# A hybrid decoder block on one core: all four compute engines run in the order written, and the attention's values move between pairs two and three

## The chip, the cores and the metric

The kernel runs on one core of one Trainium2 chip. The metric is the device time of one execution in microseconds (us). The core's engines have a queue of instructions each: TensorE (PE, matmuls; its weight loads are counted apart as PEld), VectorE (DVE), ScalarE (ACT), GpSimd (POOL) and SyncE (SP, which here only issues transfers). An engine works through its queue in the order in which the built program holds it; semaphores make it wait for others. PSUM is the memory that PE writes and that DVE and ACT read.

## What is computed

One layer, 256 tokens of width 1024. A norm, one projection to all streams, two token mixers side by side (softmax attention with 8 heads, and the RWKV-7 delta rule with 8 heads of 64), gates, and one output projection with a norm:

```python
h = rmsnorm(x, norm_pre[l])
proj = jnp.einsum('bsd,de->bse', h, w_in[l])
aq, ak, av, az, rw_stream, rz, g_att, g_rw = split_cols(proj, IN_WIDTHS)
ya = moba_attention(heads_a(aq), heads_a(ak), heads_a(av)) * silu(az)
rs, ksr, vs, wd, ad = split_cols(token_shift_mix(rw_stream, rw_mu[l]), ...)
w_log = -softplus(-(rw_w0[l] + tanh(wd) @ rw_w_up[l])) - 0.5
a = sigmoid(rw_a0[l] + ad @ rw_a_up[l])
...
# rwkv7_scan, for each token: S_t = S_{t-1} diag(w_t) + (S_{t-1} (-kk_t)) (kk_t * a_t)^T + v_t k_t^T ; o_t = S_t r_t
u = sigmoid(g_att) * (ya @ w_up_att[l]) + sigmoid(g_rw) * (yb @ w_up_rw[l])
x = x + rmsnorm(u @ w_out[l], norm_post[l])
```

With 256 tokens there is one block of keys, so the attention is causal softmax attention with ALiBi.

## The kernel before

The weights lie in DRAM as blocks of 128x1024 in the order in which they are used. Each block is loaded to `wraw` (SP queue), cast to a rounded high part `whi` on ACT (L123), and the rest `wlo` is the difference, made on DVE (L124). A block of output features is then 24 matmuls of 128x256 in triples (L137 to L139): high weights times high input, high times low, low times high. `wblock` keeps four split blocks ready, so the split of block n+3 is written at the start of block n. There are four buffers for each part, so that split waits until PE is through with block n-1.

Beside this stream run the small products of the two mixers, as generators in three lanes: `rw` (lora, the four pairs of RWKV heads, the inverse, the chunks), `att` (scores, softmax, values) and `nm` (norms of the chunks). In `proj_tile` there are three marks in each block (after k = 2, 4 and 7), at which `pump` gives every lane its rate, and a lane whose credit reaches 1 runs its next generator to the next `yield`. R_SUB, R_ATT and R_CH are such rates; a `yield` alone is one more step, so a step without work puts distance between a product and its inputs.

The stages: the opening (input norm, transposes, first three blocks, L150 to L215), wda and lora, then for p in 0 to 3 the blocks k, r and v of a pair. `pair_phase` (L373 to L438) makes decays by a scan (L378) and exps (L381, L384), the operands kap, km, ar, BK and rk, the bonus product L407, the products L422 to L427, and copies them out through masks (L434). Then the attention's values (`av_phase`, L613), eight blocks for q and k with the scores L629 between, twelve for the gates and z, four for the attention's gate. `inverse_phase` inverts 64 matrices of 32x32 at once, one substitution step (L478, L480) for each row, and moves the result through DRAM (dx, dt) into X64; L501 and L511 complete it. `chunks_phase` then runs four chunks in sequence: L524, L552, L562, L539.

What sets the order: only the opening stands under `manual_schedule`, where ACT, DVE, PE and POOL keep the order in which the code is written. For the rest a scheduler orders each engine's instructions by its own estimate of when they are ready, with a raised priority for the weight splits, the shifts and the evacuations (`hp`).

```python
cast = nc.scalar.copy(out=hi[:, a:b], in_=raw[:, a:b])
nc.vector.tensor_tensor(out=lo[:, a:b], in0=raw[:, a:b], in1=hi[:, a:b], op=ALU.subtract)
```

Of the kernel before, what the change touches and what calls it, by code (L numbers as in the profile page):

```python
# [16 lines left out]
P = 128  # L17
# [10 lines left out]
DMA_SLOTS, DMA_SLOTS2 = 10, 16  # L28
# [4 lines left out]
R_ATT, R_SUB, R_CH = 0.107, 0.75, 0.8  # L33
# [10 lines left out]
def block_kernel(ctx: ExitStack, tc: tile.TileContext, x, wp, pv, lora, npost, out):  # L44
# [102 lines left out]
    first = [wfetch(halves=n == 0) for n in range(4)]  # L147
    started = [mmps() for _ in range(3)]
    ET = mybir.EngineType
    with tc.manual_schedule(engines={ET.Activation, ET.DVE, ET.PE, ET.Pool}):  # L150

        for i in range(2):
# [5 lines left out]
            normed = nc.gpsimd.tensor_tensor(out=r, in0=r, in1=mhalf[:, 0:1], op=ALU.pow)  # L158
# [7 lines left out]
        x_scale(0, 0, 512, nc.vector)  # L166
        x_scale(0, 512, D, nc.scalar)
        x_scale(1, 0, 384, nc.vector)
        x_scale(1, 384, 768, nc.scalar)
        x_scale(1, 768, D, nc.vector)  # L170
        omu = ct([P, 13], "omu")
        nc.vector.tensor_scalar(out=omu, in0=pvt[:, PV_MU:PV_MU + 13], scalar1=-1.0, scalar2=1.0, op0=ALU.mult, op1=ALU.add)
        oka = ct([P, 4], "oka")
        nc.vector.tensor_scalar(out=oka, in0=pvt[:, PV_KA:PV_KA + 4], scalar1=-1.0, scalar2=1.0, op0=ALU.mult, op1=ALU.add)
        two = twops()
        banks = [two[:, 0], two[:, 1]] + [smps() for _ in range(3)]
        place = [(0, 0), (1, 0), (2, 0), (2, 1), (3, 0), (3, 1), (4, 0), (4, 1)]
        xps = [banks[b][:, h * T:(h + 1) * T] for b, h in place]

        def x_tr(i, j):  # L180
            nc.tensor.transpose(out=xps[j][:, i * P:(i + 1) * P], in_=xt[i][:, j * P:(j + 1) * P], identity=ident)

        def x_evac(j):
            nc.scalar.activation(out=hh[:, j, :], in_=xps[j], func=AF.Identity, scale=pvc(PV_NPRE, j))
            nc.vector.scalar_tensor_tensor(out=hl[:, j, :], in0=xps[j], scalar=pvc(PV_NPRE, j), in1=hh[:, j, :],  # L185
                                           op0=ALU.mult, op1=ALU.subtract)

        def mm_hi(n, k):
            ws = first[n][1][:, k * P:(k + 1) * P]
            nc.tensor.matmul(out=started[n][:, 0:T], lhsT=ws, rhs=hh[:, k, :], start=(k == 0), stop=False)  # L190
            nc.tensor.matmul(out=started[n][:, 0:T], lhsT=ws, rhs=hl[:, k, :], start=False, stop=False)  # L191
# [6 lines left out]
        for i in range(2):  # L198
            for j in range(KD):
                x_tr(i, j)  # L200
        nc.vector.tensor_copy(out=first[0][1][:, 0:512], in_=first[0][0][:, 0:512])
        for j in range(5):
            x_evac(j)
            mm_hi(0, j)
            if j == 1:
                nc.vector.tensor_copy(out=first[0][1][:, 512:D], in_=first[0][0][:, 512:D])
        nc.scalar.copy(out=first[1][1], in_=first[1][0])
        for j in range(5):
            mm_hi(1, j)
        for j in range(5, KD):  # L210
            x_evac(j)
            mm_hi(0, j)
            mm_hi(1, j)
        nc.scalar.copy(out=first[2][1], in_=first[2][0])
        mm_lo(0)  # L215
        for k in range(KD):
            mm_hi(2, k)
        mm_lo(1)
        mm_lo(2)
        split_3 = wsplit(first[3], 0, 1024)  # L220
    ready.append(first[3][1:])
    nc.sync.dma_start(out=lor, in_=lora.rearrange("r (n c) -> r n c", n=2))
# [68 lines left out]
    bonv = ct([P, NP, T], "bonv")  # L291
    nc.gpsimd.memset(SVE[0:64, 0], 0.0)
# [5 lines left out]
    rnt = ct([P, NP, NCH], "rnt")  # L298
# [74 lines left out]
    def pair_phase(p):  # L373

        k2 = tg()
# [6 lines left out]
        nc.gpsimd.tensor_copy(out=Gc[:, p], in_=Gl[:, :, C:C + 1])  # L382
# [21 lines left out]
        yield  # L404
        mm = nc.tensor.matmul
# [27 lines left out]
        for sc, kd, sct, kr in ((scs[:, 0], ARE, SCE, LH[1]), (scs[:, 1], ARO, SCO, LH[0])):  # L433
# [14 lines left out]
    def inverse_phase():  # L448

        dn = dram.tile([64, 32, 32], F32, name="dn")  # L450
        dx, dt_ = (dram.tile([64, 32, 32], F32, name=n) for n in ("dx", "dt"))
        for q in range(4):
            o = 32 * (q % 2)
            nc.sync.dma_start(out=dn[16 * q:16 * q + 16].rearrange("b s t -> s b t"),
                              in_=[SCE, SCO][q // 2][32 * q:32 * q + 32, :, :, o:o + 32].rearrange("s p c t -> s (p c) t"))
        nc.vector.reciprocal(out=rn2, in_=rn2)
        nc.vector.tensor_copy(out=rnt[0:64], in_=rn2[:, 0])
        nc.sync.dma_start(out=rnt[64:128], in_=rn2[:, 1])
# [6 lines left out]
        fl = tt([P, 32, 32], "slot")[0:64]  # L465
        nc.gpsimd.dma_start(out=fl, in_=dn)
        tb = tt([P, 32, 32], "slot")[0:64]
        nc.gpsimd.memset(tb, 0.0)
        nc.gpsimd.memset(tb.rearrange("b s t -> b (s t)")[:, 0:1024:33], 1.0)
        for c in range(DMA_SLOTS):  # L470
            if c < NCH - 1:
                bkt_phase(c)
            yield
# [8 lines left out]
        yield 1.0  # L482
        xb = tt([P, 32, 32], "slot")[0:64]
# [62 lines left out]
    def chunks_phase():  # L546
# [3 lines left out]
        for c in range(NCH):  # L550
            u = p4(smps())
            one_group([mm(out=u[fs, p, :], lhsT=X64[fs, p, c, :], rhs=wsb[fs, p, :], start=True, stop=True)  # L552
                       for p in range(NP) for h, fs, AR, SV, UV, SC in (EV, OD)])
            for h, fs, AR, SV, UV, SC in (EV, OD):
                nc.vector.tensor_tensor(out=UV[fs, c], in0=u[fs], in1=rnt[fs, :, c:c + 1].broadcast_to([64, NP, C]), op=ALU.mult)
# [8 lines left out]
            for h, fs, AR, SV, UV, SC in (EV, OD):  # L564
                gc = Gc[fs, :, c, :].broadcast_to([64, NP, C])
# [31 lines left out]
    yah = ct([P, NP, T], "yah", F32R)  # L597
    yal = ct([P, NP, T], "yal", F32R)
# [164 lines left out]
    def main():  # L763
# [28 lines left out]

        zg = ct([P, 3, NP, T], "BK")
# [5 lines left out]
        att.drain()  # L799
        for p in range(NP):  # L800
# [3 lines left out]
            split(at, yah[:, p, :], yal[:, p, :])  # L804
# [13 lines left out]
        for j in range(0, KD, 2):  # L818
# [3 lines left out]
            up_pair(j, yah, yal, up_att_done)  # L822
# [70 lines left out]
    finish(1, 3)  # L893


def pack(inputs):
# [11 lines left out]
    blocks += [wide(w, 1024, b) for b in range(4)]  # L908
# [44 lines left out]
```

## Time and profile before

| | before |
|---|---|
| median of 3 runs | 255.26 us (254.19 to 256.28) |
| the profiled execution | 255.23 us |
| its span, first to last instruction | 253.5 us |
| mean granted clock of PE | 0.983 |
| PE busy | 238.7 us |
| DVE / ACT / POOL busy | 181.2 / 149.4 / 32.8 us |

The span is the time from the first to the last instruction of the core; the 1.7 us around it are start and end. Busy is the union of an engine's instructions, and a matmul's record is longer than its distance to the next one, since they are pipelined. The clock is granted at one of two levels, 1.2 and 2.4 GHz, told as 0.5 and 1.0. In the row of waits, "PE smps L407 <- DVE gen L403" says that PE stood before its L407, which writes a PSUM tile named smps, until DVE had done L403.

### The profile page before, as it was taken

To read this page: it belongs to the slowest core of one execution; us is meant where nothing else is said; L and a number is where in the kernel's file an instruction comes from. 1 tells how busy PE (TensorE), PEld (TensorE's weight loads), DVE (VectorE), ACT (ScalarE), POOL (GpSimd) and SP (SyncE) were. 2 spreads that over 40 slices of the span, in tenths; PEclk is the share of its full clock that TensorE was granted. 3 is DMA by queue.
4 is the path that set the end of the run, shared out by engine and by line. 5 is a ranking of instruction groups with operands and counts; after the bars stand their busy time and mean duration, and the time that the engine had idled before them with its cause. 6 is when DMAs were issued, how large, how long until landed. Compare 5 with 4: busy or idle time off the path is not lost.

```text
span 253.5 us, 5779 instructions
## 1 busy us (share of the span) xinstructions
PE 238.7 (94%) x2283; PEld 220.8 (87%) x2283; DVE 181.2 (72%) x370; ACT 149.4 (59%) x291; POOL 32.8 (13%) x74
## 2 busy tenths in 40 slices
PE   8799998799999999999999999999997999999990
PEld 5599998798879899989899999899896999988890
DVE  2677747789894256999999277987777666998243
ACT  4676899286553767778598565763334443573241
POOL 2735000012120520000001500000112100000000
PEclk9979999799999999999999999999999999999998
DMA  6825955956578692552625958334226566442022
GB/s 231 352 67 153 376 176 175 263 177 178 125 193 257 145 356 89 172 165 87 202 100 162 272 160 288 130 107 155 82 78 217 211 200 206 168 152 98 3 74 93
DMA packets 19500, 43.68 MB, mean 172 GB/s; under 512 B 7536, under 2 KB 8688, under 8 KB 19472
## 3 DMA queue, kind: packets, MB, share of 16 engines
q1 hardware_dynamic: 18336, 41.30, 50.4%
q0 software_dynamic: 704, 1.71, 2.6%
q8 instruction: 18, 0.29, 0.5%
q10 hardware_dynamic: 432, 0.29, 0.4%
q14 instruction: 10, 0.08, 0.1%
HBM read 37.90 MB, written 1.84 MB: 157 GB/s over the span
## 4 chain that ended last, share of the span: by engine, by line
PE 78%; DVE 8%; ACT 5%; issue 4%; DMA 2%; POOL 1%; DVEq 0%; SPq 0%; ACTq 0%; POOLq 0%
PE mmps L137 17%; PE mmps L138 16%; PE mmps L139 16%; PE mmps L853 9%; PE mmps L613 3%; DVE wlo L124 2%; ACT whi L123 2%; DMA slot<-in_x_dram 2%; PE mmps L191 1%; PE twops L629 1%; PE smps L654 1%; POOL rv L581 1%; PE smps L663 1%; PE mmps L190 1%; PE twops L422 1%
## 5 line engine op out<-in xcount | busy, mean ns | idle before, releaser
L137 PE MATMUL mmps<-hh,whi 128*128 128x256 f32 x336 | 96.6, 288 | 2.2 <-DVE k L274 2.2
L139 PE MATMUL mmps<-hh,wlo 128*128 128x256 f32 x336 | 95.1, 283 | 0.0
L138 PE MATMUL mmps<-hl,whi 128*128 128x256 f32 x336 | 95.1, 283 | 0.0
L124 DVE TENSOR_TENSOR wlo<-wraw,whi 128x1024 fp32r<-128x1024 f32 x58 | 71.3, 1232 | 25.2 <-ACT whi L123 25.1
L123 ACT CAST whi<-wraw 128x1024 fp32r<-128x1024 f32 x58 | 60.8, 1048 | 41.6 <-PE mmps L138 26.7
L137 PEld LDWEIGHTS mmps<-hh,whi 128*128 128x128 f32 x336 | 63.9, 190 | 3.5 <-DVE k L274 2.4
L138 PEld LDWEIGHTS mmps<-hl,whi 128*128 128x128 f32 x336 | 63.9, 190 | 0.3
L139 PEld LDWEIGHTS mmps<-hh,wlo 128*128 128x128 f32 x336 | 63.8, 190 | 0.2
L478 DVE SCALAR_TENSOR_TENSOR gen<-slot,rnf 64x31 f32<-64x31 f32 (+15 forms) x31 | 12.2, 392 | 0.7
L480 DVE TENSOR_TENSOR slot<-slot,gen 64x31 f32<-64x31 f32 (+15 forms) x31 | 10.4, 334 | 0.7
L581 POOL TENSOR_TENSOR rv<-rv,mhalf 128x4 f32<-128x4 f32 x4 | 4.2, 1052 | 41.8 <-DVE rv L580 41.8
L137 PE MATMUL mmps<-yah,whi 128*128 128x256 f32 x32 | 9.2, 287 | 0.0
L139 PE MATMUL mmps<-slot,wlo 128*128 128x256 f32 x32 | 9.1, 283 | 0.0
L137 PE MATMUL mmps<-slot,whi 128*128 128x256 f32 x32 | 9.1, 283 | 0.0
L138 PE MATMUL mmps<-slot,whi 128*128 128x256 f32 x32 | 9.1, 283 | 0.0
L139 PE MATMUL mmps<-yah,wlo 128*128 128x256 f32 x32 | 9.0, 281 | 0.0
L138 PE MATMUL mmps<-yal,whi 128*128 128x256 f32 x32 | 9.0, 281 | 0.0
L859 DVE TENSOR_TENSOR SCE<-mmps,X 128x512 f32<-128x512 f32 (+1 forms) x5 | 2.9, 584 | 8.2 <-ACT ar L858 8.2
L858 ACT ACTIVATE ar<-mmps 128x512 f32<-128x512 f32 (+1 forms) x5 | 2.6, 514 | 10.2 <-PE mmps L853 10.2
L191 PE MATMUL mmps<-hl,whi 128*128 128x256 f32 x24 | 7.7, 343 | 0.6 <-DVE hl L185 0.2
L190 PE MATMUL mmps<-hh,whi 128*128 128x256 f32 x24 | 7.7, 341 | 0.2
L191 PEld LDWEIGHTS mmps<-hl,whi 128*128 128x128 f32 x24 | 5.5, 229 | 1.4 <-DVE hl L185 1.4
(260 smaller groups left out, 498.7 us busy)
## 6 DMA issues: line engine op xcount, KB each, us to landing
wraw<-in_wp_dram SPq DMA_DIRECT2D x64, 512.0 KB, 3.9
slot<-in_x_dram SPq DMA_DIRECT2D x2, 512.0 KB, 4.0
wraw<-in_wp_dram SPq DMA_DIRECT2D x2, 256.0 KB, 5.5
gz<-in_lora_dram SPq DMA_DIRECT2D x1, 512.0 KB, 8.2
ARE<-ar SPq DMA_DIRECT2D x4, 128.0 KB, 3.2
ARO<-ar SPq DMA_DIRECT2D x4, 128.0 KB, 3.2
bonv<-gen SPq DMA_DIRECT2D x8, 64.0 KB, 2.8
ARE<-SCE SPq DMA_DIRECT2D x4, 128.0 KB, 2.3
```

The costliest lines, as they stand in the source:

```text
L123: cast = nc.scalar.copy(out=hi[:, a:b], in_=raw[:, a:b])
L124: nc.vector.tensor_tensor(out=lo[:, a:b], in0=raw[:, a:b], in1=hi[:, a:b], op=ALU.subtract)
L137: nc.tensor.matmul(out=o, lhsT=lh, rhs=rh, start=first, stop=False)
L138: nc.tensor.matmul(out=o, lhsT=lh, rhs=rl, start=False, stop=False)
L139: nc.tensor.matmul(out=o, lhsT=ll, rhs=rh, start=False, stop=last)
L190: nc.tensor.matmul(out=started[n][:, 0:T], lhsT=ws, rhs=hh[:, k, :], start=(k == 0), stop=False)
L191: nc.tensor.matmul(out=started[n][:, 0:T], lhsT=ws, rhs=hl[:, k, :], start=False, stop=False)
L478: nc.vector.scalar_tensor_tensor(out=pr, in0=fl[:, s, s + 1:32].unsqueeze(2).broadcast_to([64, n, s + 1]), scalar=rnf[:, s:s + 1], in1=tb[ ...
L480: nc.vector.tensor_tensor(out=tb[:, s + 1:32, 0:s + 1], in0=tb[:, s + 1:32, 0:s + 1], in1=pr, op=ALU.add)
L581: nc.gpsimd.tensor_tensor(out=rv, in0=rv, in1=mhalf, op=ALU.pow)
L613: nc.tensor.matmul(out=pa[i], lhsT=a[:, k, ts], rhs=w[:, wsl], start=(k == 0 and n == 0), stop=(k == KD - 1 and n == 2))
L853: nc.tensor.matmul(out=ps, lhsT=a[:, k, ts], rhs=w[:, wsl], start=(k == 0 and m == 0), stop=(k == KD - 1 and m == 2))
```

## The change

Everything after the opening comes under `manual_schedule` too, for ACT, DVE, PE and POOL (SP's transfers are still ordered by the scheduler). So the order of the code becomes the order of the queues, and the generators are cut finer: more `yield`s, other rates. R_PAIR (0.9 of a step for each mark) is new, R_ATT rises from 0.107 to 0.16, R_SUB from 0.75 to 0.8, and R_CH falls from 0.8 to 0.5. The slots that separate the inverse's parts go from 10 and 16 to 8 and 9. The attention's values (the four wide blocks) follow pair 1 instead of pair 3, and `rw.drain()` before the inverse is gone. Line numbers shift: L378 is L400 after the change, L403 is L425, L407 is L430, L422 is L446, L434 is L458, L446 is L481, L480 is L515, L484 is L521, L501 is L535, L524 is L557, L552 is L585.

Beside the order:
- the opening is written in other steps (both norms first, four groups of features, six small bf16 products `keep_warm` between the first transposed features);
- the lora's tanh is written by ACT into both halves, where two transfers moved one half before, and its split moves from POOL to DVE;
- `Gc` is made by an exp on ACT instead of a copy on POOL;
- the masked diagonal blocks go to DRAM (`dn`) pair by pair, 16 transfers instead of 4;
- BK of the first three chunks is scaled by the decay, 12 activations of 128x192 (L471), so that the state update becomes one addition to `dec`, made earlier; in chunk 0 it is a copy;
- the norm factors `rnt` are gone: one multiply L519 (64x1024) puts them into the inverse, and the two multiplies at L496 and the factor in L555 go;
- the chunk's u has a PSUM tile for each half of the heads.

```diff
-DMA_SLOTS, DMA_SLOTS2 = 10, 16
+DMA_SLOTS, DMA_SLOTS2 = 8, 9
-R_ATT, R_SUB, R_CH = 0.107, 0.75, 0.8
+R_PAIR, R_ATT, R_SUB, R_CH = 0.9, 0.16, 0.8, 0.5
...
+        def keep_warm():
+            nc.tensor.matmul(out=started[2][:, 0:T], lhsT=wz[:, 0:P], rhs=wz, start=True, stop=True)
...
     def pair_phase(p):
+        if p == 0:
+            yield R_PAIR
...
-        nc.gpsimd.tensor_copy(out=Gc[:, p], in_=Gl[:, :, C:C + 1])
+        nc.scalar.activation(out=Gc[:, p], in_=c4(cs)[:, :, C - 1:C], func=AF.Exp, scale=-DECAY_SCALE)
...
         nc.vector.scalar_tensor_tensor(out=rk, in0=rs_[p], scalar=pvc(PV_RK, p), in1=km, op0=ALU.mult, op1=ALU.mult)
+        yield
         yield
...
+            nc.sync.dma_start(out=dn[16 * q + 4 * p:16 * q + 4 * p + 4].rearrange("b s t -> s b t"),
+                              in_=[SCE, SCO][q // 2][32 * q:32 * q + 32, p, :, o:o + 32])
+    def bk_decay(c):
+        for p in range(NP):
+            nc.scalar.activation(out=BK[:, p, c, :], in_=BK[:, p, c, :], func=AF.Identity, scale=Gc[:, p, c, :])
...
         for c in range(DMA_SLOTS):
             if c < NCH - 1:
-                bkt_phase(c)
+                bk_decay(c)
+            if 2 <= c < NCH + 1:
+                bkt_phase(c - 2)
+            if c == NCH:
+                bkt_done.append(c)
             yield
...
+        nc.vector.tensor_tensor(out=tb, in0=tb, in1=rnf.unsqueeze(2).broadcast_to([64, 32, 32]), op=ALU.mult)
         xb = tt([P, 32, 32], "slot")[0:64]
         nc.vector.tensor_copy(out=xb, in_=tb.rearrange("b t j -> b j t"))
...
-            u = p4(smps())
+            ue, uo = p4(smps()), p4(smps())
...
-                nc.vector.tensor_tensor(out=dst, in0=s[fs], in1=SV[fs, c], op=ALU.add)
-                nc.vector.tensor_tensor(out=dst, in0=dst, in1=gc, op=ALU.mult)
+                if c:
+                    nc.vector.tensor_tensor(out=dst, in0=s[fs], in1=dec[fs], op=ALU.add)
+                else:
+                    nc.vector.tensor_copy(out=dst, in_=s[fs])
...
-        yield from av_phase()
-        rw.drain()
+            if p == 1:
+                yield from av_phase()
...
+        while not bkt_done:
+            rw.step()
...
+    order = tc.manual_schedule(engines={ET.Activation, ET.DVE, ET.PE, ET.Pool})
+    order.__enter__()
     for _ in main():
         pass
...
+    order.__exit__(None, None, None)
```

On DVE, between the products of pair 2 and the bonus product of pair 3, the queue before held (scan L378, masks L434, rk L403; wlo is a weight split, gen a buffer of the pair):

```order
L378 SCALAR_TENSOR_TENSOR gen<-rst,qT 128x256
L394 TENSOR_TENSOR ar<-r,Gl 128x4x64
L393 SCALAR_TENSOR_TENSOR ar<-gen,Gl 128x4x64
L434 TENSOR_TENSOR SCE<-twops,msk 128x512
L429 TENSOR_SCALAR rn_337<-smps 64x2x4
L434 TENSOR_TENSOR SCO<-twops,msk 128x512
L390 TENSOR_TENSOR gen<-gen,k 128x256
L399 TENSOR_TENSOR gen<-gen,kT 128x256
L398 TENSOR_TENSOR BK<-gen 128x4x64
L124 TENSOR_TENSOR wlo<-wraw,whi 128x1024
L400 TENSOR_TENSOR BK<-gen 128x4x64
L403 SCALAR_TENSOR_TENSOR gen<-r,pvt,gen 128x256
```

And it holds after the change (scan L400, masks L458, rk L425):

```order
L458 TENSOR_TENSOR SCO<-twops,msk 128x512
L300 SCALAR_TENSOR_TENSOR v<-mmps,pvt,v 128x255
L124 TENSOR_TENSOR wlo<-wraw,whi 128x1024
L400 SCALAR_TENSOR_TENSOR gen<-rst,qT 128x256
L412 TENSOR_TENSOR gen<-gen,k 128x256
L415 SCALAR_TENSOR_TENSOR ar<-gen,Gl 128x4x64
L416 TENSOR_TENSOR ar<-r,Gl 128x4x64
L124 TENSOR_TENSOR wlo<-wraw,whi 128x1024
L420 TENSOR_TENSOR BK<-gen 128x4x64
L421 TENSOR_TENSOR gen<-gen,kT 128x256
L422 TENSOR_TENSOR BK<-gen 128x4x64
L425 SCALAR_TENSOR_TENSOR gen<-r,pvt,gen 128x256
```

The scan and the two products for ar stood ahead of the masks and now stand behind them, and behind a shift and a weight split; before the products for BK there is a second split.

On ACT, in the stretch of the q and k blocks, the queue before held (L446 copies transposed BK out of PSUM):

```order
L123 CAST whi<-wraw 128x1024
L783 ACTIVATE qT<-mmps,qsc 128x256
L462 COPY gen<-smps 32x64
L446 COPY BKt<-smps 128x256 x6
L123 CAST whi<-wraw 128x1024
L787 COPY kT<-mmps 128x256
L123 CAST whi<-wraw 128x1024
L783 ACTIVATE qT<-mmps,qsc 128x256
L643 ACTIVATE lg,l<-lg,mn 128x128
```

And after the change, where the same copy is L481, and pt is a copy of transposed attention weights:

```order
L824 COPY yal<-mmps 128x256
L123 CAST whi<-wraw 128x1024
L498 COPY gen<-smps 32x64
L471 ACTIVATE BK<-BK,Gc 128x192 x12
L481 COPY BKt<-smps 128x256 x2
L694 COPY pt<-smps 128x384 x2
L680 ACTIVATE lg,l<-lg,mn 128x128
L681 ACTIVATE lg,l<-lg,mn 128x256
L683 ACTIVATE lg<-lg,l 128x128
L684 ACTIVATE lg<-lg,l 128x256
L680 ACTIVATE lg,l<-lg,mn 128x128
L681 ACTIVATE lg,l<-lg,mn 128x256
```

The twelve scalings L471 stand in one piece ahead of the copies, and the softmax of a pair of attention heads stands behind them as one piece too.

On DVE at the end of the inverse, the queue before held (slot is the inverse, X the tile that the transfers fill):

```order
L480 TENSOR_TENSOR slot<-slot,gen 64x31
L124 TENSOR_TENSOR wlo<-wraw,whi 128x1024
L484 COPY slot<-slot 64x1024
L124 TENSOR_TENSOR wlo<-wraw,whi 128x1024 x2
L496 TENSOR_TENSOR X_329<-X_329,rnt 32x16x32 x2
```

And after the change:

```order
L515 TENSOR_TENSOR slot<-slot,gen 64x31
L124 TENSOR_TENSOR wlo<-wraw,whi 128x1024
L519 TENSOR_TENSOR slot<-slot,rnf 64x1024
L521 COPY slot<-slot 64x1024
L727 TENSOR_TENSOR gen<-mmps,gen 128x256
L843 TENSOR_TENSOR gz<-gz,gen 128x256
```

The multiply L519 is new and stands between the last split and the copy; the multiplies on X behind the transfers are gone.

## Rows read from the trace of the kernel before

**Rows 1.** Page, part 1 (PE: busy, share, instructions) and the clock row of part 2, 40 slices.

```profile
PE 238.7 (94%) x2283; PEld 220.8 (87%) x2283; DVE 181.2 (72%) x370; ACT 149.4 (59%) x291; POOL 32.8 (13%) x74
...
PEclk9979999799999999999999999999999999999998
```

**Rows 2.** Busy time by stretch of the span; columns are in the row's own words.

```profile
0.00:27.30 27.30, 24.48 (x162) 21.39 (x163) 16.98 (x32) 16.18 (x28) 12.61 (x40) 0.94 0.61 216
27.30:76.80 49.50, 46.76 (x437) 42.54 (x436) 37.99 (x69) 34.85 (x62) 5.49 (x12) 0.97 0.68 199
76.80:149.30 72.50, 72.20 (x658) 68.04 (x657) 52.62 (x129) 50.40 (x114) 9.89 (x17) 1.00 0.60 181
149.30:200.00 50.70, 47.98 (x708) 45.06 (x707) 39.43 (x80) 25.74 (x52) 4.83 (x5) 1.00 0.47 163
```

**Rows 3.** Waits of PE: line waited for, us in total, times, longest.

```profile
PE mmps L137 <- DVE k L274: 2.2, 1, 2.2
PE smps L524 <- DVE SVO L568: 1.5, 2, 1.1
...
PE smps L407 <- DVE gen L403: 0.2, 1, 0.2
...
PE smps L407 <- ACT whi L123: 0.2, 1, 0.2
```

**Rows 4.** Timeline of PE around 46 us and at 83.8: start, us, instruction, count.

```profile
45.76 0.38 PE L137 MATMUL mmps<-hh,whi 128*128 128x256 f32 x1 [2.23 <-DVE k L274]
...
46.10 0.28 PE L139 MATMUL mmps<-hh,wlo 128*128 128x256 f32 x1
46.22 0.28 PE L137 MATMUL mmps<-hh,whi 128*128 128x256 f32 x1
...
47.59 0.41 PE L138 MATMUL mmps<-hl,whi 128*128 128x256 f32 x1
...
49.72 0.41 PE L139 MATMUL mmps<-hh,wlo 128*128 128x256 f32 x1
...
83.82 1.39 PE L445 MATMUL smps<-ident,BK 64*128 64x64 f32 x16 [0.30 <-ACT gen L462]
```

**Rows 5.** Groups of DVE by form: count, busy us, mean ns, idle before.

```profile
L124 DVE TENSOR_TENSOR wlo<-wraw,whi 128x1024 fp32r<-128x1024 f32 x58 | 71.3, 1232 | 25.2 <-ACT whi L123 25.1
...
L434 DVE TENSOR_TENSOR SCE<-twops,msk 128x512 f32<-128x512 f32 x4 | 2.7, 684 | 0.8 <-PE twops L422 0.8
L378 DVE TENSOR_TENSOR_SCAN gen<-rst,qT 128x256 f32<-128x256 f32 x4 | 2.7, 680 | 0.0
...
L390 DVE TENSOR_TENSOR gen<-gen,k 128x256 f32<-128x256 f32 x4 | 1.7, 416 | 0.0
```

**Rows 6.** Groups of ACT by form.

```profile
L123 ACT CAST whi<-wraw 128x1024 fp32r<-128x1024 f32 x58 | 60.8, 1048 | 41.6 <-PE mmps L138 26.7 <-issue 8.8 <-DMA wraw<-in_wp_dram 2.8
...
L644 ACT ACTIVATE lg<-lg,mn 128x256 f32<-128x256 f32 x8 | 4.0, 499 | 0.1
...
L643 ACT ACTIVATE lg<-lg,mn 128x128 f32<-128x128 f32 x8 | 3.2, 398 | 4.3 <-DVE mn L638 4.3
...
L387 ACT ACTIVATE gen<-k,pvt 128x256 f32<-128x256 f32 x4 | 2.0, 496 | 0.0
...
L446 ACT COPY BKt<-smps 128x256 f32<-128x256 f32 x6 | 1.9, 372 | 0.0
```

**Rows 7.** Timeline of DVE and POOL behind the last substitution step.

```profile
136.32 1.23 DVE L124 TENSOR_TENSOR wlo<-wraw,whi 128x1024 fp32r<-128x1024 f32 x1
137.47 1.13 DVE L484 COPY slot<-slot 64x1024 f32<-64x1024 f32 x1
...
143.53 2.58 POOL L490 DMA_DIRECT2D X<-dx  x4 [1.98 <-DMA dx<-slot]
```

**Rows 8.** Transfers by source and destination: KB each, median us from issue to landing.

```profile
dx<-slot POOLq DMA_DIRECT2D x1, 256.0 KB, 4.1
X<-dx POOLq DMA_DIRECT2D x4, 64.0 KB, 5.5
```

More of the change, by code (lines that the diff above doesn't have):

```diff
@@ L174, in block_kernel @@
[L174 to L181, printed above, removed]
@@ L193, in mm_lo, with mm_hi @@
+        def mm_hi(n, k, r):
+            nc.tensor.matmul(out=started[n][:, 0:T], lhsT=first[n][1][:, k * P:(k + 1) * P], rhs=r[:, k, :], start=(k == 0 and r is hh), stop=False)
         def mm_lo(n):
@@ L207, in block_kernel @@
[L207 to L213, printed above, removed]
+        def keep_warm():
+            nc.tensor.matmul(out=started[2][:, 0:T], lhsT=wz[:, 0:P], rhs=wz, start=True, stop=True)
+        x_norm(0)
+        omu = ct([P, 13], "omu")
+        nc.vector.tensor_scalar(out=omu, in0=pvt[:, PV_MU:PV_MU + 13], scalar1=-1.0, scalar2=1.0, op0=ALU.mult, op1=ALU.add)
@@ new lines, in block_kernel @@
+        normed = x_norm(1)
+        x_scale(0, 0, 512, nc.vector)
+        x_scale(0, 512, D, nc.scalar)
+        x_tr(0, range(KD))
+        w_hi(0, nc.vector, 0, 512)
+        x_scale(1, 0, 384, nc.vector)
+        x_scale(1, 640, D, nc.scalar)
+        x_scale(1, 384, 640, nc.vector)
+        x_tr(1, range(KD))
+        for u in units:
+            for r, f in ((hh, x_hi), (hl, x_lo)):
+                for j in u:
+                    f(j)
+                if u[0] == 1 and r is hh:
+                    nc.scalar.copy(out=first[0][1][:, 512:D], in_=first[0][0][:, 512:D])
+                for j in u:
+                    mm_hi(0, j, r)
+                    if j < 3:
+                        keep_warm()
+            if u[0] == 0:
+                w_hi(1, nc.vector, 0, 512)
+                oka = ct([P, 4], "oka")
+                nc.vector.tensor_scalar(out=oka, in0=pvt[:, PV_KA:PV_KA + 4], scalar1=-1.0, scalar2=1.0, op0=ALU.mult, op1=ALU.add)
+            if u[0] == 3:
+                for r in (hh, hl):
+                    for k in range(4):
+                        mm_hi(1, k, r)
@@ L214, in block_kernel @@
+        nc.scalar.copy(out=first[1][1][:, 512:D], in_=first[1][0][:, 512:D])
+        for r in (hh, hl):
+            for k in range(4, KD):
+                mm_hi(1, k, r)
         nc.scalar.copy(out=first[2][1], in_=first[2][0])
+        for r in (hh, hl):
+            for k in range(KD):
+                mm_hi(2, k, r)
         mm_lo(0)
-        for k in range(KD):
-            mm_hi(2, k)
         mm_lo(1)
         mm_lo(2)
-        split_3 = wsplit(first[3], 0, 1024)
+        wsplit(first[3], 0, 1024)
@@ L221, in block_kernel @@
+        LH = (slice(0, 64), slice(64, 128))
+        lrs = ct([P, 2, 512], "yah", F32R)
+        nc.scalar.copy(out=lrs, in_=lor)
+        for n in range(2):
+            nc.vector.tensor_tensor(out=lrs[LH[1 - n], n], in0=lor[LH[1 - n], n], in1=lrs[LH[1 - n], n], op=ALU.subtract)
     ready.append(first[3][1:])
-    nc.sync.dma_start(out=lor, in_=lora.rearrange("r (n c) -> r n c", n=2))
     with tc.issue_after(normed.ins):
@@ L448, in inverse_phase @@
     def inverse_phase():
-        dn = dram.tile([64, 32, 32], F32, name="dn")
+        yield 1.0
         dx, dt_ = (dram.tile([64, 32, 32], F32, name=n) for n in ("dx", "dt"))
[L452 to L455, printed above, removed]
+        tb = tt([P, 32, 32], "slot")[0:64]
+        nc.gpsimd.memset(tb, 0.0)
+        nc.gpsimd.memset(tb.rearrange("b s t -> b (s t)")[:, 0:1024:33], 1.0)
+        fl = tt([P, 32, 32], "slot")[0:64]
+        nc.gpsimd.dma_start(out=fl, in_=dn)
         nc.vector.reciprocal(out=rn2, in_=rn2)
-        nc.vector.tensor_copy(out=rnt[0:64], in_=rn2[:, 0])
-        nc.sync.dma_start(out=rnt[64:128], in_=rn2[:, 1])
+        yield
+        yield
         rp = smps()
@@ L907, in pack @@
             blocks.append(feat(c0 + p * P))
-    blocks += [wide(w, 1024, b) for b in range(4)]
+        if p == 1:
+            blocks += [wide(w, 1024, b) for b in range(4)]
     for p in range(NP):
```

96 lines of the change are left out of this document (40 added, 56 removed).

## The prediction

> **What bounds the kernel now.** I read the page's first parts first: TensorE (PE) is busy for 238.7 us of the 253.5 us span, and VectorE (DVE) and ScalarE (ACT) for 72% and 59% [rows 1]. Then the span cut at the ends of the opening, of the four pairs, of the inverses' stage and of the chunks [rows 2]: PE's missing time is 2.74 us between 27.3 and 76.8, 0.30 up to 149.3 and 2.72 up to 200, in all 5.76. So PE bounds every stage, and the other engines have time to spare, but only on average. PE's waits come next [rows 3]: one of 2.2 us on a shift of DVE, and two on state updates of the chunks; the bonus products L407 wait 0.4 together. Last I read PE's timeline right after the first of these [rows 4]: matmuls start 0.12 us apart at 46.10, and from 47.59 to 49.72 ten of them take 2.13, 0.21 each. The page's clock row shows the same dip to 0.79 in its eighth slice [rows 1]; that is the lower of the two levels, 1.2 GHz, and it came after the wait. From 46.57 to 50.12 that is 3.55 us at half the rate, so about 1.75 us are lost.
>
> The run in the profile took 255.23 us, 0.03 under the median of 255.26, so I work with it. A measurement here tells about 1% from no change.
>
> **What the change can win at most.** If the new order left PE no waits after the opening, the 5.76 us and the 1.75 us would go. In the opening (0 to 27.3) the clock is 0.94 [rows 2], which means 0.06 x 27.3 = 1.6 us lost at the low level; the six small products and the earlier transposes address that, but the next block's split now stands behind the tanh and lora work in ACT's and DVE's queues. Bounds 0 and 1.6; I take the middle, 0.8, having no row for either end. So the best case is 255.23 - 5.76 - 1.75 - 0.80 = 246.9 us.
>
> **What it costs.** Before, the scheduler could place a small product later or a weight split earlier than it was written. Now an instruction stands where it is written, and each weight split (cast on ACT, subtraction on DVE) is written at the start of a block, where it must wait for the buffer of the block before. So neither engine can run ahead of PE by more than that, and everything written between two splits must fit in the block's time. A block is 24 matmuls 0.117 apart (0.12 in the rounded starts of rows 4), 2.81 us. The durations are from [rows 5, 6]; back to back, one instruction starts 0.08 us before the former's record ends (the split at 136.32 takes 1.23, and the copy behind it starts at 137.47 [rows 7]), so I take 0.08 off each.
>
> The bonus product of a pair (L407, now L430), with the last pair (pair 3) as the worked case. After the products of pair 2, PE has two blocks, 5.62 us, before L430 of pair 3. DVE must in that time do, in this order: the norm's maximum 0.1, two masks 1.20, a shift 0.40, a split 1.15, the scan 0.60, 0.34 for km, 0.34 twice for ar, a split 1.15, 0.34 three times for BK, 0.40 for rk: 7.0 us with no wait at all. Waits come on top: the first split needs ACT, which has two state copies, a shift and a cast before it (0.30 + 0.30 + 0.39 + 0.97, so 2.1 instead of 1.7), and km waits behind the scan for five activations on ACT (Gl, Gc, the second exp, kap and km, 0.29 to 0.42 each: 1.8). With these the product rk ends 10.0 us after the pair's products. PE waits 10.0 - 5.6 = 4.4 us. The same walk gives 9.4 against 5.6 for pair 2 (3.8), 10.2 against 7.0 for pair 0, where the sigmoids and a table load stand in the chain and the attention's values don't help yet (3.2), and 1.1 for pair 1, which has the 11 us of values in front of it. Sum 12.5. In the trace of before the L407 waits together are 0.4 us [rows 3], because rk was placed ahead of other work and L407 behind a longer stretch of blocks.
>
> The scores of attention pair 0 stand in front of the masks of pair 3 with their reciprocals on DVE waiting for exps on ACT: 1.5. Those of the last pair wait 0.6 in the same way.
>
> The decay of BK, 12 new activations of 128x192 (L471), is the next place. No row shows that form; by the 128x128 and 128x256 forms (0.40, and 0.37 to 0.50 [rows 6]) each costs 0.29 to 0.42, and I take 0.35, the middle: 4.2 us together, bounds 3.5 and 5.0. They stand in one piece in ACT's queue, in front of the transposes' copies. From the end of the block that is evacuated at L824, ACT has: that copy 0.30, a cast 0.97, L498 0.30, L471 4.2, two copies 0.6, two of L694 0.8, two softmaxes 3.0 to 4.4 by the forms of 128x128 and 128x256 and the sums read out after the exps (4.2), L820 0.4, a cast 0.97, a copy 0.3, sum 13.0; the reciprocals between bring it to 13.3. PE meanwhile has 13 triples of 0.35 (4.6), sixteen transposes, which take 1.39 in the trace [rows 4], and eleven other small ones (scores, transposes of weights of attention, L496), at an estimated 0.15 between the 0.09 of those transposes and 0.2: 1.6. Sum 7.6. Its next transposes (L480) need a PSUM tile that these copies empty, so it waits 13.3 - 7.6 = 5.7.
>
> The inverse's results. One new multiply L519 (64x1024, near the copy's 1.13 [rows 7]) precedes the copy, and the slots behind go from 16 to 9 marks, which is three blocks. Before, the copy ended at 138.60, the last loads into X were issued from 143.53 to 146.11 and took 5.5 us [rows 7, 8], so they landed about 11.4 to 12 after the copy; that was hidden, with no wait of PE on it. Now the split, L519 and the copy end 5.0 us after the block begins, the same transfers (dt now behind dx, one after the multiply) land 12 later, at 17, and PE is at L535 after 3 blocks and 3 triples, 9.5. It waits 7.5.
>
> By the Trainium skill (DMA: Bandwidth & Descriptors, section "Anatomy of one DMA — SWDGE (gpsimd) path") a transfer from this queue takes 2.0 us plus its bytes over 436 KB per us: as an estimate 2.6 us for dx and 2.15 for a piece of X. The rows have 4.1 and 5.5, with weights moving at the same time, so here the measurement decides; by the page both hops would be 4.9 us shorter, this wait 2.6 and the sum 275.6.
>
> The first chunk. The gate z of four pairs is written in one piece after the last value gate: on ACT and DVE by turns some 0.4, 0.4 and 0.5 (the forms of 128x256) with nothing between that PE needs [rows 5, 6], 1.35 x 4 = 5.4. Behind it ACT has the cast and the copy of the chunk's input (L560): L585 is ready 9.2 us after the block, PE after 3.4. It waits 5.8. In the trace of before PE shows no such wait.
>
> The rest I cost at nothing: the two tanh transfers gone (no PE wait is on them), u in two PSUM tiles and the state as one addition (the two waits on SVO, 1.5, are in the 5.76 already), Gc as an exp (0.3, counted in the pairs), dn by pairs (16 transfers for 4, hidden by the pairs themselves; without cover 0.65 each, an issue's time in rows 7, though on SP), two table loads fewer (off the path; without that, a gain).
>
> Sum: 246.9 + 12.5 + 1.5 + 0.6 + 5.7 + 7.5 + 5.8 = 280.5 us.
>
> **The rivals.** *Clock*: as above, but each wait of over 2 us is followed by a low stretch like the one at 47 us, 1.75 each. There are eight waits: 14 us more, 294.5. I leave it out of the sum, because most stretches that follow end in another wait, whose end other engines set. *Half*: ACT and DVE are further ahead at the start of each stretch than I walked them, the splits are absorbed, and half of the 33.6 us shows: 263.7. For it: my walk puts every split at the latest time, and a wait once taken lets the others catch up. Against it: DVE's own 7.0 against 5.6 holds without any wait of its own. *Dense, on the other side*: three blocks' look-ahead covers all chains, PE never starves, the order only removes the old waits: 246.9. It decides as soon as the new waits sum to less than 8.3 us. For it: on average ACT and DVE have over a quarter of the time free [rows 1] and 25 us of DVE's idle time is spent waiting for casts [rows 5]; against it: that idle time can't be used in advance when the order is fixed. *The order does little*, waits of about 8 us replace the old ones: 255.
>
> **How the numbers follow.** My walk 0.63, the clock on top 0.11, half 0.14, about equal 0.04, dense 0.08. The likeliest is 280.5. The 8-in-10 range takes in half of the clock case and the half case, and leaves out the lower ones: 258 to 295. Faster by over 1%: 0.08; within 1%: 0.04; slower: 0.88.
>
> **What would show it.** In the changed kernel's profile: PE's idle time ahead of L430 of 3.2, 1.1, 3.8 and 4.4 us, released by rk on DVE; 5.7 ahead of L480, released by copies on ACT; 7.5 ahead of L535 by the loads into X; 5.8 ahead of L585. PE's busy share falls from 94% to about 85%. If instead PE waits less than 2 us at the pairs and at L535, the walk is wrong at its root, which is that the other engines can't get ahead; if the waits are there and the span is shorter, the floor is wrong.

## The result and the profile after

The changed kernel takes 301.21 us (median of 4 runs, 300.3 to 302.12) against 254.74 of before in the same comparison: ratio 1.1815, interval 1.1762 to 1.1869. It is slower by 18%, where 10% were forecast, and outside the range, which ended at 295. The profiled execution took 302.12 us, of which the span is 300.4; for the kernel before it was 255.23 and 253.5.

The page of the changed kernel, parts 1 and 2, answers to [rows 1]:

```profile
PE 249.7 (83%) x2289; PEld 229.2 (76%) x2289; DVE 185.7 (62%) x366; ACT 151.3 (50%) x311; POOL 26.4 (9%) x68
...
PEclk9999979999797997799999998576899999999998
```

PE's busy share has fallen to 83%, though it does the same products and only the six small ones more; and it is busy 11 us longer. The clock row now has eleven slices below 0.9 ahead of its last, where it had two. The stretches of the span, as in [rows 2] (opening, pairs, attention, end of the inverse and chunks, last stages):

```profile
0.00:26.60 26.60, 22.84 (x168) 20.18 (x169) 19.66 (x39) 17.66 (x31) 8.71 (x37) 1.00 0.66 238
26.60:97.50 70.90, 57.44 (x503) 52.65 (x503) 41.49 (x70) 34.61 (x67) 3.26 (x9) 0.93 0.58 172
97.50:178.70 81.20, 75.36 (x654) 70.18 (x653) 51.06 (x125) 49.91 (x119) 4.78 (x9) 0.96 0.39 126
178.70:235.00 56.30, 39.62 (x554) 36.73 (x554) 32.62 (x61) 21.50 (x44) 7.04 (x10) 0.82 0.35 110
235.00:293.60 58.60, 54.42 (x427) 49.44 (x423) 38.21 (x68) 26.82 (x48) 2.59 (x3) 1.00 0.39 131
```

Idle time is the second number less the third: 13.5 us between the opening and pair 3's products, 5.8 in the attention, 16.7 around the inverse's end and the first chunk, 4.2 at the end. Before, it was 2.74, 0.30 and 2.72 [rows 2]. PE's waits, as in [rows 3]:

```profile
PE smps L430 <- DVE gen L425: 13.5, 4, 4.3
PE smps L535 <- DMA X<-dt: 10.1, 2, 6.7
PE smps L585 <- issue: 5.4, 1, 5.4
PE smps L480 <- ACT BKt L481: 3.2, 1, 3.2
PE mmps L137 <- DVE BK L766: 2.3, 2, 1.7
PE mmps L895 <- DVE BK L766: 1.7, 1, 1.7
...
PE mmps L139 <- DVE wlo L124: 1.3, 2, 0.8
PE mmps L137 <- DVE gen L727: 1.2, 1, 1.2
PE smps L691 <- ACT BKt L481: 1.1, 1, 1.1
...
PE twops L446 <- DVE mn L677: 0.9, 1, 0.9
PE mmps L137 <- ACT whi L123: 0.3, 1, 0.3
```

The single largest is L430, the bonus product of a pair, four times, 13.5 us together. Its counterpart L407 waited 0.4 before. The wait that led the list before (L137 on a shift of DVE) is gone.

DVE in the stretch ahead of pair 3's L430 (start, us, instruction; in brackets the idle time before it and what ended it):

```profile
83.25 0.16 DVE L453 TENSOR_SCALAR rn<-smps 64x8 f32<-64x8 f32 x1 [3.75 <-PE smps L451]
...
85.54 1.22 DVE L124 TENSOR_TENSOR wlo<-wraw,whi 128x1024 fp32r<-128x1024 f32 x1 [0.46 <-ACT whi L123]
86.69 0.69 DVE L400 TENSOR_TENSOR_SCAN gen<-rst,qT 128x256 f32<-128x256 f32 x1
89.21 0.42 DVE L412 TENSOR_TENSOR gen<-gen,k 128x256 f32<-128x256 f32 x1 [1.84 <-ACT gen L411]
...
90.51 1.23 DVE L124 TENSOR_TENSOR wlo<-wraw,whi 128x1024 fp32r<-128x1024 f32 x1 [0.20 <-ACT whi L123]
...
92.78 0.48 DVE L425 SCALAR_TENSOR_TENSOR gen<-r,pvt,gen 128x256 f32<-128x256 f32 x1
```

And PE at the end of it:

```profile
93.41 1.19 PE L430 MATMUL smps<-gen,onesb 128*128 128x256 f32 x2 [4.33 <-DVE gen L425]
```

This is the chain of the worked case. Between 83.25 and 93.26 DVE does what is written and in that order; it idles only for ACT (0.46 and 0.20 for the casts, 1.84 for km's activations behind the scan). rk ends 10.0 us after the pair's products, and PE has stood for 4.33 us.

ACT in the attention's stretch:

```profile
106.72 4.26 ACT L471 ACTIVATE BK<-BK,Gc 128x192 f32<-128x192 f32 x12
...
117.37 0.91 ACT L481 COPY BKt<-smps 128x256 f32<-128x256 f32 x3
```

The twelve scalings L471 take 4.26 us in one piece (4.2 was the estimate), and of the copies that free PE's transposes two follow at once; the next three stand behind the softmax too and begin at 117.37.

POOL at the end of the inverse, and PE behind it:

```profile
180.28 0.54 POOL L523 DMA_DIRECT2D dx<-slot  x1 [68.03 <-DVE slot L521]
...
187.63 0.65 POOL L527 DMA_DIRECT2D X<-dx  x1
```

```profile
188.41 0.28 PE L535 MATMUL smps<-X,SCE 32*32 32x32 f32 x2 [6.72 <-DMA X<-dt]
192.04 0.26 PE L535 MATMUL smps<-X,SCO 32*32 32x32 f32 x1 [3.35 <-DMA X<-dt]
```

dx and dt are issued right after the copy L521; the last load into X is issued at 187.63. PE's first wait on these loads ends at 188.41, the second at 192.04.

### The profile page after: what moved, and what is told of

It reads as the page before. It is cut to its first block, busy times and chain, and to the rows that moved or that the text cites. A ratio compares the mean times of both kernels' runs of the same rounds, so it can differ in the third digit from the quotient of the medians.

```text
span 300.4 us, 5804 instructions
## 1 busy us (share of the span) xinstructions
PE 249.7 (83%) x2289; PEld 229.2 (76%) x2289; DVE 185.7 (62%) x366; ACT 151.3 (50%) x311; POOL 26.4 (9%) x68
## 3 DMA queue, kind: packets, MB, share of 16 engines
HBM read 37.90 MB, written 1.84 MB: 132 GB/s over the span
## 4 chain that ended last, share of the span: by engine, by line
PE 54%; DVE 18%; ACT 13%; issue 7%; DMA 6%; POOL 1%; SPq 0%; DVEq 0%; ACTq 0%; POOLq 0%
PE mmps L137 11%; PE mmps L139 10%; PE mmps L138 10%; PE mmps L895 7%; DVE wlo L124 6%; ACT whi L123 4%; DMA X<-dt 2%; DMA slot<-in_x_dram 1%; PE smps L430 1%; PE twops L446 1%; DVE gen L513 1%; ACT BK L471 1%; PE smps L572 1%; DMA dt<-slot 1%; DMA ARE<-SCE 1%
## 5 line engine op out<-in xcount | busy, mean ns | idle before, releaser
L137 PE MATMUL mmps<-hh,whi 128*128 128x256 f32 x336 | 101.1, 301 | 1.5 <-DVE gen L727 1.2
L139 PE MATMUL mmps<-hh,wlo 128*128 128x256 f32 x336 | 97.5, 290 | 1.3 <-DVE wlo L124 1.3
L138 PE MATMUL mmps<-hl,whi 128*128 128x256 f32 x336 | 97.5, 290 | 0.0
L137 PEld LDWEIGHTS mmps<-hh,whi 128*128 128x128 f32 x336 | 66.8, 199 | 3.5 <-DVE gen L727 1.4
L139 PEld LDWEIGHTS mmps<-hh,wlo 128*128 128x128 f32 x336 | 66.6, 198 | 2.0 <-DVE wlo L124 2.0
L138 PEld LDWEIGHTS mmps<-hl,whi 128*128 128x128 f32 x336 | 66.6, 198 | 0.2
L430 PE MATMUL smps<-gen,onesb 128*128 128x256 f32 x8 | 4.3, 633 | 13.5 <-DVE gen L425 13.5
L430 PEld LDWEIGHTS smps<-gen,onesb 128*128 128x128 f32 x8 | 1.8, 280 | 14.4 <-issue 11.9
L137 PE MATMUL mmps<-slot,whi 128*128 128x256 f32 x32 | 9.3, 292 | 2.4 <-DVE BK L766 2.3
L515 DVE TENSOR_TENSOR slot<-slot,gen 64x31 f32<-64x31 f32 (+15 forms) x31 | 10.4, 335 | 1.1
L836 ACT COPY BK<-mmps 128x256 f32<-128x256 f32 x12 | 4.5, 376 | 11.9 <-PE mmps L139 11.9
L731 ACT CAST ARE<-BK 128x256 fp32r<-128x256 f32 x8 | 3.3, 406 | 13.5 <-DVE BK L767 13.5
L461 POOL MEMSET SCE<- 64x512 f32 x4 | 2.1, 522 | 87.6 <-DMA ARE<-SCE 87.6
L137 PE MATMUL mmps<-yah,whi 128*128 128x256 f32 x32 | 9.3, 291 | 0.0
```

Of the source, the lines that this page charges most:

```text
L137: nc.tensor.matmul(out=o, lhsT=lh, rhs=rh, start=first, stop=False)
L138: nc.tensor.matmul(out=o, lhsT=lh, rhs=rl, start=False, stop=False)
L139: nc.tensor.matmul(out=o, lhsT=ll, rhs=rh, start=False, stop=last)
L430: mm(out=pb[:, 0:T], lhsT=onesb, rhs=rk, start=True, stop=True)
L515: nc.vector.tensor_tensor(out=tb[:, s + 1:32, 0:s + 1], in0=tb[:, s + 1:32, 0:s + 1], in1=pr, op=ALU.add)
L731: nc.scalar.copy(out=hi, in_=src)
```

## The experiments

Two theories stood against each other. The first: the written order on ACT and DVE makes short chains late, and PE pays for each wait and for the low clock around it. The second: the other edits (decay on ACT, L519, fewer marks, values after pair 1) cost the time, whatever the order.

**e1_scheduled.** All edits, order written only in the opening:

```diff
-    order = tc.manual_schedule(engines={ET.Activation, ET.DVE, ET.PE, ET.Pool})
-    order.__enter__()
...
-    order.__exit__(None, None, None)
```

> The changed kernel with all its edits, but the written order held only in the opening, as before; the rest is ordered by the scheduler. If the fixed order makes the loss: 250 to 262 us, and PE's wait ahead of L430 under 2 us in all instead of 13.5. If the other edits (decay on ACT, the multiply L519, fewer slots, the values after pair 1) make it: 285 to 302 us, with the waits at L535 and L585 still there.

251.54 us against 255.42 of before, ratio 0.9845 (0.9804 to 0.9885); no wait at L430, none at L535 and L585. So the fixed order makes the whole loss, and the edits without it (the new opening among them) are a gain of 1.5%. Two waits of 2.1 us are left in it, at L496 and L666. What leads to the first is in SP's queue and ACT's:

```profile
77.12 0.91 SPq L464 DMA_DIRECT2D dn<-SCO  x2
...
78.78 0.60 SPq L117 DMA_DIRECT2D wraw<-in_wp_dram  x1
...
80.65 1.57 SPq L117 DMA_DIRECT2D wraw<-in_wp_dram  x3
```

```profile
83.30 1.05 ACT L123 CAST whi<-wraw 128x1024 fp32r<-128x1024 f32 x1 [2.73 <-DMA wraw<-in_wp_dram]
```

Seven issues stand in a row from 74.46 up to the weights at 78.78, three of them into dn, 0.5 to 0.6 us each, and three more weight blocks follow only at 80.65. ACT's cast waited for such weights until 83.30.

**e2_before_ordered.** The kernel before, with the same three lines around its `main` and its last stage, and no other edit.

> The kernel before, with the written order for all four engines after the opening and no other edit. If the fixed order makes the loss: 295 us or more, since here the products stand closer behind their inputs than in the changed kernel; waits of PE at L407, L422 and L524 of over 2 us each. If the order is harmless by itself: 252 to 262 us.

315.0 us, ratio 1.2323 (1.2268 to 1.2378). Of the waits that were expected, those at L524 are 3.9 us together and those at L422 2.0; the largest is at L407:

```profile
PE smps L407 <- DVE gen L403: 13.4, 4, 4.8
```

The order alone costs 23% of the time; the edits, made for this order, took back some 5% of before's time (1.2323 to 1.1815).

**e5_pe_only** and **e6_act_dve.** The changed kernel with the order fixed after the opening for PE alone, and for ACT and DVE alone:

```diff
-    order = tc.manual_schedule(engines={ET.Activation, ET.DVE, ET.PE, ET.Pool})
+    order = tc.manual_schedule(engines={ET.PE})
```

```diff
-    order = tc.manual_schedule(engines={ET.Activation, ET.DVE, ET.PE, ET.Pool})
+    order = tc.manual_schedule(engines={ET.Activation, ET.DVE})
```

> The changed kernel, but after the opening only PE keeps the written order; ACT, DVE and POOL are ordered by the scheduler. If the loss comes from chains on ACT and DVE that the written order makes late: 255 to 268 us, with L430's wait under 5 us of the 13.5 and no wait at L585. If it comes from products that PE meets too early: 285 us or more.

> The changed kernel, but after the opening only ACT and DVE keep the written order; PE and POOL are ordered by the scheduler. If the loss comes from the chains on ACT and DVE: 280 to 300 us. If it comes from products that PE meets too early: 252 to 270 us, since PE then does weight products ahead of them.

PE alone: 255.92 us, ratio 0.9978 (0.9942 to 1.0013), no measurable difference from before. ACT and DVE alone: 286.6, ratio 1.1172 (1.1095 to 1.1248). What the order itself costs is read against e1_scheduled (0.9845), which has the same edits: 1.3% of before's time for PE alone, 13.3% for ACT and DVE, 19.7% for all four engines. L430 waits once in the first:

```profile
PE smps L430 <- DVE gen L425: 3.5, 1, 3.5
```

In the second there is no row of L430 at all; PE now waits for evacuations and in the chunks:

```profile
PE mmps L137 <- ACT yah L820: 5.8, 3, 3.1
PE smps L585 <- issue: 5.5, 1, 5.5
```

So most of the loss comes with the order on ACT and DVE. A scheduler that may move PE's products takes away the pairs' waits, but not those for ACT's and DVE's late work. Some 5% come only when all four are fixed. Which of ACT and DVE counts more was not tried, nor was POOL's order apart from the others'.

**e4_fill.** Products whose results are overwritten, in front of the waiting ones, so that PE is not idle there:

```diff
+    def fill(ps, n):
+        for _ in range(n):
+            nc.tensor.matmul(out=ps, lhsT=ident, rhs=dist, start=True, stop=True)
...
         pb = smps()
+        fill(pb[:, 0:T], (7, 5, 8, 9)[p])
```

> The changed kernel with extra products in PE's queue ahead of L430, L535 and L585 (29, 21 and 11 of 128x256, results overwritten), about as long as the waits there. The waits' ends are set by other engines, so only the clock can gain. If the low clock after waits costs what the sum left out: PE's clock near 0.97 and 290 to 296 us. If the waits alone make the time: 299 to 304 us.

293.33 us, ratio 1.1474 (1.1438 to 1.151). The clock row:

```profile
PEclk9999999999999999899999999999999999999998
```

Ahead of the last one only one slice is below 0.9, at the wait ahead of L480, where nothing was filled in. Adding 61 products of no use made the kernel faster by 0.034 of before's time, 8.7 us (by the two intervals, about 7 to 10). In the changed kernel the three longest of the six low stretches in the middle of the span, and the sum over all six (PE's clock is the 0.50):

```profile
116.75:123.58 6.83, 5.78 (x28) 5.67 (x29) 2.45 (x2) 3.23 (x7) 0.00 (x0) 0.50 0.25 80
185.02:198.67 13.65, 6.91 (x127) 6.51 (x129) 4.43 (x7) 2.79 (x5) 3.21 (x5) 0.50 0.48 139
205.50:212.33 6.83, 3.98 (x29) 3.89 (x30) 4.01 (x6) 3.84 (x8) 0.00 (x0) 0.50 0.21 77
sum 37.56, PE 25.84 PEld 24.29 DVE 16.29 ACT 9.86 POOL 3.21; mean PE 4.31 PEld 4.05 DVE 2.72 ACT 1.64 POOL 0.54
```

In 37.56 us at 0.50 PE was busy for 25.84, so about half of that, 12.9 us, is the low clock's, as an estimate. The stretch at 116.75 lies at L480; the five others, where products were filled in, hold 20.06 of the 25.84, or 10.0 us.

**e3_slots16.** `DMA_SLOTS2` 16 instead of 9.

> The changed kernel with 16 marks instead of 9 behind the inverse's transfers. 7 marks are 6.6 us, so the wait at L535 falls from 10.1 to 2 to 4 us. If a wait's price is its length and the low clock around it: 290 to 294 us. If the lower clock there is set by something else or the chunks' later end costs the same at the end of the kernel: 298 to 303 us.

299.23 us, ratio 1.1736 (1.1662 to 1.1809): within the intervals no clear gain. The wait at L535 fell as expected, but others came:

```profile
PE smps L543 <- DVE ysb L539: 4.3, 1, 4.3
...
PE smps L535 <- DMA X<-dt: 2.1, 1, 2.1
```

The distance was moved into other waits: L543 now waits for DVE's copy of the result of L535, the end of the chunks comes late (1.9 us at L625), and the low clock lasts from 190.7 to 207.7. So this wait's price can't be read from its length.

**e10_gatez.** The gate z of pair p written behind the split in block p of the attention's gate:

```diff
             split(at, yatt[0][:, p, :], yatt[1][:, p, :])
-            yield
...
-        for p in range(NP):
             z = tg()
             after(nc.scalar.activation(out=z, in_=zg[:, 0, p, :], func=AF.Sigmoid), last_soft)
...
+            yield
```

> The changed kernel in its written order, with the gate z made pair by pair in the four blocks of the attention's gate, instead of in one piece behind them. If L585 waits for this piece in ACT's and DVE's queues: its wait of 5.4 us falls under 1.5, and 293 to 297 us with the low clock there. If it waits for the loads into X or for L543's copies: the wait stays over 3 us and 299 to 302 us.

293.81 us, ratio 1.15 (1.1431 to 1.1569). The wait at L585 is 1.5 us instead of 5.4, that at L535 8.5 instead of 10.1, and no low stretch follows at 205 us. In the changed kernel ACT stands there, taking turns with DVE, and L560 comes at the end:

```profile
202.62 0.51 ACT L853 ACTIVATE gz<-gen,pvt 128x256 f32<-128x256 f32 x1 [0.51 <-DVE gen L852]
...
207.89 0.36 ACT L560 COPY gen<-smps 128x256 f32<-128x256 f32 x1
```

**e11_pairs.** Three more `yield`s between rk and L430.

> The changed kernel in its written order, with three more marks between rk and the bonus product L430 in each pair, 2.8 us of weight products each. If PE only meets L430 too early: the four waits fall from 13.5 to 3 to 4.5 us, three low clock stretches go, and 286 to 292 us as long as the chunks still end ahead of the last stage. If the splits in between bind, and the chain moves with the marks: waits of 10 us or more remain and 298 to 304 us.

286.87 us, ratio 1.1216 (1.1139 to 1.1293), 15 us faster than the changed kernel. Line numbers are 3 higher here:

```profile
PE smps L538 <- DMA X<-dt: 5.8, 2, 4.3
PE smps L433 <- DVE gen L425: 4.6, 3, 2.9
```

Two marks were too few for chains of 9 to 10 us; with five the waits fall to 4.6. The waits at L535's counterpart fell too, from 10.1 to 5.8, without an edit there; the wait on L727's counterpart grew from 1.2 to 3.7.

**e7_tail.** In the last stage the split of a tile written one tile later:

```diff
+            if late:
+                split(*late.pop())
...
-            split(g, us[0][:, j, :], us[1][:, j, :])
+            late.append((g, us[0][:, j, :], us[1][:, j, :]))
```

> The changed kernel, in the last stage before the output product (L766, L767) the split of a tile written one tile later, so that ACT's cast of the next weights isn't behind DVE's products. The waits on L766 (2.3 and 1.7 us) should go. If these are a price of the written order as at the pairs: 296 to 298.5 us. If the stage is bound by something else: 300 to 302 us.

297.82 us, ratio 1.1616 (1.1566 to 1.1667). This is a wait that the prediction did not have. DVE in the changed kernel's last stage, and ACT beside it:

```profile
265.58 1.23 DVE L124 TENSOR_TENSOR wlo<-wraw,whi 128x1024 fp32r<-128x1024 f32 x1 [0.52 <-ACT whi L123]
266.72 0.42 DVE L766 TENSOR_TENSOR BK<-mmps,BK 128x256 f32<-128x256 f32 x1
...
270.72 1.23 DVE L124 TENSOR_TENSOR wlo<-wraw,whi 128x1024 fp32r<-128x1024 f32 x1 [0.53 <-ACT whi L123]
```

```profile
267.63 0.41 ACT L731 CAST ARE<-BK 128x256 fp32r<-128x256 f32 x1 [2.09 <-DVE BK L767]
...
269.64 1.05 ACT L123 CAST whi<-wraw 128x1024 fp32r<-128x1024 f32 x1
```

A weight split needs ACT's cast, ACT's cast stands behind a cast of a product, that behind DVE's product, and this behind the split before: one round takes 5.14 us (265.58 to 270.72), where a block's matmuls take 2.81. Three blocks of look-ahead absorb part of it, and 4.0 us of PE's waits are left; with the split one tile later they are 0.5 + 0.5.

**e8_dn_pool.** e1_scheduled with the transfers to dn on POOL's queue:

```diff
-            nc.sync.dma_start(out=dn[16 * q + 4 * p:16 * q + 4 * p + 4].rearrange("b s t -> s b t"),
+            nc.gpsimd.dma_start(out=dn[16 * q + 4 * p:16 * q + 4 * p + 4].rearrange("b s t -> s b t"),
```

> The run e1_scheduled, with the 16 transfers to dn issued from POOL's queue instead of SP's, where each issue takes 0.6 us and weights are issued behind them. If that is why ACT's cast waited 2.7 us for weights at 83.3 and PE 2.1 at L496: 248 to 250.5 us. If these waits come from the chain of pair 3 itself: 251 to 253 us.

247.02 us, ratio 0.963 (0.9585 to 0.9674): faster than both kernels.

```profile
PE 235.9 (96%) x2289; PEld 218.4 (89%) x2289; DVE 181.1 (74%) x366; ACT 151.3 (62%) x311; POOL 35.8 (15%) x84
...
PEclk9999999999999999999999999999999999999997
```

PE has no wait of over 1 us after its first products, and no low clock before the end. Its execution in the profile took 246.82 us.

**e9_av_late.** e8_dn_pool with the values behind pair 3 again.

> The run e8_dn_pool, with the attention's values behind pair 3 again instead of pair 1. If the values between the pairs give the chains of pairs 2 and 3 the time that they lacked: 249 to 252 us with a wait at a pair. If the scheduler covers the pairs anyway: 246 to 248.5 us.

248.66 us, ratio 0.9734 (0.9685 to 0.9782). The values' new place is worth about 1% of before's time in this version, and the time lies between the two ranges: the wait at a pair did not come (L430 0.2 us), and 1.3 us stand at L625 instead. Where the rest goes stays open.

**e12_opening.** The kernel before with the new opening alone.

> The kernel before with the new opening alone (its order, the small bf16 products, the lora's split in it). By the sum: 0 to 1.6 us gained there, 253 to 255.5. If the clock's low stretch at 12.5 us and the wait at 43 us both hang on the opening: 250 to 252 us.

251.36 us, ratio 0.9848 (0.9796 to 0.99): 1.5%, or 3.9 us. Both low stretches ahead of the last slice are gone, and PE's wait on L274 (here L300) is 0.5 us instead of 2.2. This edit alone is as good as all edits of e1_scheduled.

## Why the prediction was wrong

The direction was right, and so was the mechanism of the waits; the size was not. The sum left out two terms: the low clock around the waits, and the waits of the last stage.

**What PE gains at most** was right: 246.9 us, and e8_dn_pool, where PE has no wait left, took 246.82 in its profile. That run shows what a PE without waits takes, and not that this order could give it. Inside the figure, 0.8 for the opening, 2.2 for the wait at 45 us and 1.75 for the dip behind it were counted apart, 4.75 in all; e12_opening shows that all three hang on the opening and gives 3.9, so that the agreement to 0.1 us is in part luck.

**The walk of the waits** was right in its places and, at the pairs, in its sizes, but for pair 1. Pairs 3.2, 1.1, 3.8 and 4.4 against 3.1, 2.3, 3.8 and 4.3 measured; L480 with the transposes L691 5.7 against 4.3; the first chunk 5.8 against 5.4; the scores 1.5 and 0.6 against 0.9 and none; X 7.5 against 10.1. In sum 33.6 against 34.2, and this closeness is luck: L480 and the scores were 2.6 us too large, X 2.6 too small. The term of X was too small, though the transfers took what I took: 12.0 us from the copy's end to the end of PE's last wait (180.0 to 192.04), as against 12. What failed is the place of the copy. I let DVE begin L519 when the block's split was done, but the substitution, with a weight split in each block, fills DVE's queue (whether its new rate is to blame was not tried):

```profile
170.00:180.00 10.00, 9.12 (x75) 8.71 (x74) 9.58 (x21) 3.09 (x4) 0.00 (x0) 1.00 0.59 204
...
177.71 1.21 DVE L519 TENSOR_TENSOR slot<-slot,rnf 64x1024 f32<-64x1024 f32 x1
178.96 1.03 DVE L521 COPY slot<-slot 64x1024 f32<-64x1024 f32 x1
```

DVE is busy for 9.58 of these 10 us. So the copy ended 1.7 us before PE came to L535 (188.41 less 6.72), not 4.5, and 10.1 us were left to wait. By the Trainium skill (DMA: Bandwidth & Descriptors, section "Anatomy of one DMA — SWDGE (gpsimd) path") dx and dt would take 2.6 us each and a load into X 2.15, as estimates from its fit. This trace has 2.9 for dx and 3.7 for dt, and the six loads are issued 0.65 us apart or later and land 4.0 to 4.1 us after issue in the median. So the short wait of 2.6 that came out by the page did not appear.

**The clock** is the step that failed: "I leave it out of the sum, because most stretches that follow end in another wait, whose end other engines set." The runs show 12.9 us in its place: the waits at pairs 0, 2 and 3, at L480, L535 and L585 had a low stretch around each (the 2.3 us at pair 1 had none), and the six hold 25.84 us of PE's work at half speed. The reason given did not hold either: the filled places hold 10.0 us of this, and e4_fill got 8.7 back, so later waits absorbed little. The rival that priced the clock, 294.5, was nearer, but in part by luck: it counted eight waits of over 2 us, where the sum has six (three pairs, L480, X, the first chunk), which at 1.75 each are 10.5 us and 291.0. Measured were six stretches of 2.2 us on average.

**The last stage** was left out: the loop of splits and products there, which is the same mechanism as at the pairs, costs 4.0 us of waits, of which e7_tail leaves 1.0. Some 2.8 us more are small waits of PE in the same trace: 1.3 for DVE's split, 1.2 for the attention's gate (L727) and 0.3 for a cast.

With these the sum is 246.9 + 34.2 + 12.9 + 6.8 = 300.8, against 302.12 in the profiled execution; the rest is not assigned. The profiles agree: beside e8_dn_pool, which has the same products and no such waits, PE is busy 13.8 us longer (249.7 and 235.9) and idle 41.5 us longer (50.7 and 9.2 of the spans of 300.4 and 245.1).

Of what "I cost at nothing", one edit is shown to cost something: dn by pairs. It was put at 0.65 us an issue without cover. In e1_scheduled, where the pairs' waits are gone, it delays weights, and its move to POOL is worth 2.2% of before's time. That the pairs' waits hide it in the changed kernel is not shown; no run moved it there. The others were not tried one by one.

The rival "dense" needed the waits to sum to less than 8.3 us. It was wrong for the written order, and is what the scheduled version with the transfers moved does.

## What to carry to other kernels

Before an order is fixed by hand on engines that also feed the bottleneck, add up each helper's queue between two of its weight splits: once a chain of short products takes longer than the marks between it and its consumer, the bottleneck waits by the difference, and that can be walked from durations: here to 0.1 us at three pairs, while pair 1 was off by 1.2, L480 by 1.4 and the loads into X by 2.6, where DVE came to the chain's start later than walked. Price an idle TensorE twice, for the wait and for the products that it then does at 1.2 GHz; here these were 41.0 us of waits and about 12.9 for the clock. And try an edit apart from the order it came with: here the order cost 50 us and hid edits worth 4, as much as the new opening alone, or 9 with one kind of transfer moved.

## What had not been expected of the hardware

Sixty-one products of no use in front of three kinds of waits made the kernel 8.7 us faster, since PE's clock stayed at 2.4 GHz there. And sixteen small transfers, 0.5 to 0.6 us each to issue, delayed weights that stood behind them in SP's queue enough to make PE wait; from POOL's queue, which had time, they did not.
